# 32x32 turns on VectorE inside the triangular inverses, and a two-pass fp32 output product in the mixer

## Chip, cores and metric
One core of a Trainium2 chip runs one program of 53121 instructions. The time is device microseconds of one execution; lower is better.

## The reference, cut to what matters
Two blocks in sequence on 256 tokens of width 2048, all in float32. The first block's mixer joins an attention half and a state-space half and multiplies them by one output matrix:

```
attn = rms_norm(nsa_attention(...), attn_out_norm)          # 256 x 1024
ssm = mamba2_ssd(...)                                       # 256 x 1024
return jnp.concatenate([attn, ssm], axis=-1) @ w_out        # 2048 x 2048
```

The second block has two recurrent branches (a gated delta rule with 8 heads, and RWKV-7 with 16 heads). The kernel works them in chunks of 128 tokens, and each chunk of each head needs the inverse of a 128x128 lower triangular matrix with a unit diagonal.

## The kernel before, in words
**Products.** Large products keep fp32 accuracy with a faster format: `split` turns a raw 128x1024 weight tile into `whi` (ScalarE, a rounding copy, L280) and `wlo` (VectorE, the remainder, L284), and the activations are kept as a like pair. `mm3` (L291 to L293) adds three products of such halves; `mm2` (L299, L300) does the same with two matmuls where both halves of the activations lie side by side.

**Weights.** `raw` (L261 to L267) loads a tile over SP's queue into four buffers, and while the pool `more` is there, every third tile into two others. `split` has two sets of `whi` and `wlo`, and a third set while the pool `third` is there (it is there in the mixer).

**Order.** The program is written as generators. `fill` takes one step of the product at the head of a queue (load and split one tile, then the matmuls of the tile before it) and, at a set rate, a step of a background generator (`ada_rest`: a 128x1024 tile of the modulation matrix is loaded, VectorE multiplies it in, L355). `weave` mixes such steps into chains of small dependent work. A planner then orders the instructions of each engine; each engine and each DMA queue works in that order.

**Mixer's output product.** `tm` runs over 4 groups of 512 columns. Per group and half it takes 4 weight tiles, each with 2 inner blocks by 2 token halves, so 16 products with 512 columns. The half on the attention's output `aT` runs beside the state-space scan (`ssd`), the half on `mT` after it; `ev_a` and `ev_m` take up the results, `ev_m` also stores them over SP's queue (L684). `chunk_T` turns 128 columns of an activation on TensorE and makes the pair (L444, L445).

**The inverses.** `inverse2` takes two matrices side by side (128x256). It starts from 2x2 squares: mask, turn on TensorE (L1798), subtract from the identity (L1800). Then, for b = 2, 4, 8, 16, 32: two products `lb` by `Y` (L1805), two turns of `Y` on TensorE into the other half of the same bank (L1807), one ScalarE copy of all 512 columns (L1809), a masked block for the next b on GpSimd (L1790), two products of the copies (L1814), and a subtraction into `Y` (L1815). A last step joins the 64x64 halves. It is called 16 times from `rwkv_pair` and 8 times from `gdn_pair`, two calls side by side.

Of the kernel before, what the change touches and what calls it, by code (L numbers as in the profile page):

```python
# [7 lines left out]
F32 = mybir.dt.float32  # L8
F32R = mybir.dt.float32r
I32 = mybir.dt.int32  # L10
U32 = mybir.dt.uint32
AF = mybir.ActivationFunctionType
ALU = mybir.AluOpType
# [5 lines left out]
S = 256  # L19
# [214 lines left out]
class K:  # L234
    def __init__(self, tc, A, at, dbg=None):
        self.tc, self.nc, self.A, self.at, self.dbg_ = tc, tc.nc, A, at, dbg
        self.n = 0
        self.pp, self.queue, self.done, self.bg = [], [], set(), []
        self.bgr, self.bgc = 1.0, 0.0
        self.side, self.later = [], [[] for _ in range(LAG)]  # L240
        self.third, self.ns = None, 0
        self.more, self.nr = None, 0

# [41 lines left out]

    def wt(self, src, n=1024, **kw):
        return self.split(self.raw(src, n), n, **kw)

    def mm3(self, out, shi, slo, mhi, mlo, start, stop):
        mm = self.nc.tensor.matmul  # L290
# [145 lines left out]
    def chunk_T(self, src, dg, hi, lo, scale, half=0):  # L436

        nc = self.nc
        if half == 0:
            self.ctb = self.bank()  # L440
        ps = self.ctb[:, half * S : half * S + S]
        for q in range(2):
            self.turn(ps[:, q * 128 : q * 128 + 128], src[q], dg and dg[q])
        nc.scalar.activation(hi, ps, AF.Copy, scale=scale)  # L444
        nc.vector.scalar_tensor_tensor(lo, ps, scale, hi.bitcast(F32), op0=ALU.mult, op1=ALU.subtract)  # L445

    def chunks_T(self, pool, x, cs, dg, hh, hl, scale, shift):

# [156 lines left out]
    def mixer(self, hp, mx, ax, hT, kvT, qT, xs, ev, scr):  # L605
        nc, tc, A = self.nc, self.tc, self.A
        hh, hl = hT[:2]
# [29 lines left out]
        self.feed(*[self.cm(A["w1cm"], j, hT, lambda j, ps: ev((2 * NP + j + 8) % 12, ps), ("x", j)) for j in range(12 - 2 * NP)])  # L637
        self.feed(*[self.tm(A["w1z"], g, hT, self.gates(xs[2]), ("z", g)) for g in range(2)])
        atp = tc.alloc_tile_pool(name="atp", bufs=1, side="right")
        aT = [self.t(atp, [128, 8, S], F32R) for _ in range(2)]  # L640
        self.until("t320")
        gate = self.t(mx, [128, 2, 48])
        nc.scalar.activation(gate, vtm[:, :, 256:304], AF.Tanh, scale=0.5)
# [13 lines left out]
        nw = self.cp("attn_norm", "cp2")  # L657
        for c in range(8):
            a = [at[:, q, c * 128 : c * 128 + 128] for q in range(2)]
            self.chunk_T(a, None, aT[0][:, c], aT[1][:, c], nw[:, c : c + 1], c % 2)  # L660
        self.dbg("aTd", aT[0].bitcast(F32))
        ax.release()

        xp = tc.alloc_tile_pool(name="x1p", bufs=1)
# [20 lines left out]

        wo = lambda h: [A["wo1"][8 * g + 4 * h + i] for g in range(4) for i in range(4)]
        for g in range(4):
            self.feed(self.tm(wo(0), g, aT, ev_a, nk=8))
        assert not self.side
        self.until(*[("x", j) for j in range(12 - 2 * NP)])  # L690
        self.flush()
        turn, mT = self.ssd(mx, xs, hp)
        self.drain()
        for g in range(4):
            self.feed(self.tm(wo(1), g, mT, ev_m, nk=8))
        self.fill(3)
        for _ in turn:
            pass
        self.dbg("mTd", mT[0].bitcast(F32))
        self.drain()  # L700
        while self.bg:
            self.step_bg()
# [251 lines left out]
    def ssd(self, mx, xs, hp):  # L954

        nc = self.nc
        V, ACT, PL = nc.vector, nc.scalar, nc.gpsimd
        tri = self.cp("tri", "ca")
        xtm, bc, zs = xs
        dt, acs, acsT, ds = self.sd  # L960
        y = zs
        ss = self.t(mx, [128, 4])

        def scan(g, hg, cbT, py):
            h = g * 8 + hg
            pa = self.bank()
            nc.tensor.matmul(pa[:, 0:256], self.ident[:16, h : h + 1].to_broadcast([16, 128]), acsT, start=True, stop=True)
            seg = self.t(mx, [128, 384], tag="seg", bufs=2)
            ACT.activation(seg[:, 0:256], pa[:, 0:256], AF.Relu, scale=-1.0, bias=acs[:, 0, h : h + 1])
            ACT.activation(seg[:, 256:384], pa[:, 128:256], AF.Relu, scale=-1.0, bias=acs[:, 1, h : h + 1])  # L970
            ACT.activation(seg, seg, AF.Exp, scale=-1.0)
            V.scalar_tensor_tensor(seg[:, 0:256], seg[:, 0:256], dt[:, 0, h : h + 1], cbT[:, 0:256], op0=ALU.mult, op1=ALU.mult)
            V.scalar_tensor_tensor(seg[:, 256:384], seg[:, 256:384], dt[:, 1, h : h + 1], cbT[:, 256:384], op0=ALU.mult, op1=ALU.mult)
            yield
            o = slice(hg * 64, hg * 64 + 64)
            xc = slice(h * 64, h * 64 + 64)
            nc.tensor.matmul(py[0][:, o], seg[:, 0:128], xtm[:, 0, xc], start=True, stop=True)
            nc.tensor.matmul(py[1][:, o], seg[:, 128:256], xtm[:, 0, xc], start=True, stop=False)
            nc.tensor.matmul(py[1][:, o], seg[:, 256:384], xtm[:, 1, xc], start=False, stop=True)
            yield  # L980

        def turns(g, mT):
            nw = self.cp("ssm_norm", "cp2")
            for c in range(4 * g, 4 * g + 4):
                a = [y[:, q, c * 128 : c * 128 + 128] for q in range(2)]
                self.chunk_T(a, None, mT[0][:, c], mT[1][:, c], nw[:, c : c + 1], c % 2)
                if c % 2:
                    yield

        for g in range(2):  # L990
            ps = self.bank()
            Bt, Ct = bc[:, g], bc[:, 2 + g]
            nc.tensor.matmul(ps[:, 0:256], Bt[:, 0:128], Ct, start=True, stop=True)
            nc.tensor.matmul(ps[:, 256:384], Bt[:, 128:256], Ct[:, 128:256], start=True, stop=True)
            cbT = self.t(mx, [128, 384], tag="cbT", bufs=2)
            V.tensor_tensor(cbT[:, 0:256], ps[:, 0:256], tri, op=ALU.mult)
            V.tensor_tensor(cbT[:, 256:384], ps[:, 256:384], tri[:, :128], op=ALU.mult)
            py = [self.bank() for _ in range(2)]
            self.fill()
            gens = [scan(g, hg, cbT, py) for hg in range(8)]  # L1000
            if g:
                gens.insert(2, turn)
            self.weave(gens, 1, 0.17)
            self.until(("z", g))
            for q in range(2):
                c = slice(g * 512, g * 512 + 512)
                t1 = self.t(mx, [128, 512], tag="yd", bufs=2)
                PL.tensor_tensor(
                    t1.rearrange("p (h d) -> p h d", h=8), xtm[:, q, c].rearrange("p (h d) -> p h d", h=8),
                    ds[:, g * 8 : g * 8 + 8, None].to_broadcast([128, 8, 64]), op=ALU.mult,  # L1010
                )
                V.tensor_tensor(t1, py[q], t1, op=ALU.add)
                V.tensor_tensor(y[:, q, c], t1, zs[:, q, c], op=ALU.mult)
                ACT.activation(t1, y[:, q, c], AF.Square, accum_out=ss[:, 2 * q + g : 2 * q + g + 1])
            r = self.rstd(mx, ss[:, g::2], 2, 512.0, 4 * EPS)
            y0, y1 = (y[:, q, g * 512 : g * 512 + 512] for q in range(2))
            ACT.activation(y0, y0, AF.Copy, scale=r[:, 0:1])
            V.tensor_scalar(y1, y1, r[:, 1:2], None, op0=ALU.mult)
            if g == 0:
                self.until(("z", 1))  # L1020
                mT = self.pair(hp, 8, "hh")
            turn = turns(g, mT)
        return turn, mT

# [326 lines left out]
    def tm(self, wd, g, hT, evac, key=None, nk=NK):  # L1351

        hh, hl = hT[:2]
        ps = [self.t(self.acc, [128, 512], tag="acc") for _ in range(2)]
        for kp in range(nk // 2):
            hi, lo = self.wt(wd[g * (nk // 2) + kp])
            yield
            for k in range(2):
                kk = 2 * kp + k
                w = slice(k * 512, k * 512 + 512)  # L1360
                for q in range(2):
                    tk = slice(q * 128, q * 128 + 128)
                    self.mm3(ps[q], hh[:, kk, tk], hl[:, kk, tk], hi[:, w], lo[:, w], kk == 0, kk == nk - 1)
        for q in range(2):
            evac(g, q, ps[q])
        self.done.add(key)

    def step_bg(self):
        while self.bg:
# [408 lines left out]
    def inverse2(self, L, res):  # L1778
# [14 lines left out]

        lm, lb = masked(1), masked(2)
        yield
        ps = self.bank()
        for i in range(2):
            nc.tensor.transpose(ps[:, T[i]], lm[:, T[i]], self.ident)  # L1798
        Y = self.r1()
        V.tensor_tensor(v2(Y), id2, v2(ps[:, 0:256]), op=ALU.subtract)  # L1800
        yield
        for b in (2, 4, 8, 16, 32):
            ps = self.bank()
            for i in range(2):
                mm(ps[:, T[i]], lb[:, T[i]], Y[:, T[i]], start=True, stop=True)  # L1805
            for i in range(2):
                nc.tensor.transpose(ps[:, U[i]], Y[:, T[i]], self.ident)  # L1807
            zx = self.r2()
            nc.scalar.activation(zx, ps, AF.Copy)  # L1809
            if b < 32:  # L1810
                lb = masked(2 * b)
            yield
            for i in range(2):
                mm(ps[:, U[i]], zx[:, U[i]], zx[:, T[i]], start=True, stop=True)  # L1814
            V.tensor_tensor(Y, Y, ps[:, 256:512], op=ALU.subtract)  # L1815
            yield
# [496 lines left out]
```

## Time and profile before
| | us |
|---|---|
| median of 3 runs | 3645.67 (3633.72 to 3649.02) |
| the profiled execution | 3638.32, span 3636.3 |
| TensorE busy | 3473.7 |
| VectorE busy | 2570.2 |
| ScalarE busy | 1692.7 |
| GpSimd busy | 397.2 |

Busy times are the union of an engine's instructions. A matmul's own duration holds its way through the array and overlaps with the next one's, so what a matmul costs in a stream is read from the distance between starts. A plain fp32 matmul shows as two matmul records.

### The profile page before, as it was taken

How to read it: one execution, taken by the hardware profiler on the slowest of the kernel's cores; microseconds unless marked ns; L12 is line 12 of the kernel's file. 1: busy time of each engine (PE TensorE's matmuls, PEld its weight loads, DVE VectorE, ACT ScalarE, POOL GpSimd, SP SyncE). 2: the span in 40 equal slices, each digit the busy share in tenths (PEclk: the TensorE clock that was granted, in tenths of full speed). 3: DMA queues.
4: the chain of work that ended last, by engine and by line, in shares of the span. 5: the costliest groups of instructions: out<-in, count | busy, mean ns of one | idle time of the engine just before them, and what ended most of it. 6: DMA issues, size and time to landing. Idle time of an engine off the chain costs nothing. (4 is left out here: it accounts for less than half of the span.)

```text
span 3636.3 us, 53121 instructions
## 1 busy us (share of the span) xinstructions
PE 3473.7 (96%) x19334; PEld 2930.2 (81%) x19334; DVE 2570.2 (71%) x4552; ACT 1692.7 (47%) x2966; POOL 397.2 (11%) x487
## 2 busy tenths in 40 slices
PE   5899988999999999999999998999999999999998
PEld 4888767888998888778887877877888888778887
DVE  7777886798887755565577668989766666665665
ACT  2355544445554444445555554333544445444444
POOL 0000010000000000000000002333223222021310
PEclk7999988999999999999999998999999999999999
DMA  8965776666556865566788755645433433444455
GB/s 334 336 225 194 251 254 209 197 196 202 161 159 207 259 190 188 183 204 206 241 283 285 248 189 202 198 152 188 147 109 112 144 129 106 140 132 151 141 176 189
DMA packets 237298, 710.46 MB, mean 195 GB/s; under 512 B 34091, under 2 KB 61804, under 8 KB 235756
## 3 DMA queue, kind: packets, MB, share of 16 engines
q1 hardware_dynamic: 207564, 672.08, 56.7%
q10 hardware_dynamic: 29472, 34.98, 2.9%
q8 instruction: 152, 2.49, 0.3%
q14 instruction: 110, 0.90, 0.1%
HBM read 673.87 MB, written 32.55 MB: 194 GB/s over the span
## 5 line engine op out<-in xcount | busy, mean ns | idle before, releaser
L284 DVE TENSOR_TENSOR wlo<-raw,whi 128x1024 fp32r<-128x1024 f32 (+1 forms) x973 | 1216.8, 1251 | 595.2 <-ACT whi L280 591.1
L280 ACT ACTIVATE whi<-raw 128x1024 fp32r<-128x1024 f32 (+1 forms) x973 | 1017.7, 1047 | 1252.1 <-PE acc L293 577.2
L299 PE MATMUL acc<-hh,whi 128*128 128x512 f32 x3328 | 1195.2, 400 | 0.7 <-DVE cT L459 0.7
L300 PE MATMUL acc<-hh,wlo 128*128 128x256 f32 x3328 | 939.1, 282 | 7.0 <-DVE wlo L284 7.0
L299 PEld LDWEIGHTS acc<-hh,whi 128*128 128x128 f32 x3328 | 626.2, 188 | 143.3 <-issue 4.5
L300 PEld LDWEIGHTS acc<-hh,wlo 128*128 128x128 f32 x3328 | 629.2, 189 | 13.1 <-DVE wlo L284 11.7
L292 PE MATMUL acc<-wlo,wh 128*128 128x512 f32 x1024 | 402.8, 393 | 6.4 <-DVE wlo L284 5.5
L293 PE MATMUL acc<-whi,wl 128*128 128x512 f32 x1024 | 400.1, 391 | 0.0
L291 PE MATMUL acc<-whi,wh 128*128 128x512 f32 x1024 | 396.9, 391 | 3.3 <-DVE ge L1345 2.8
L291 PE MATMUL acc<-whi,hh 128*128 128x512 f32 (+1 forms) x672 | 273.7, 411 | 3.2 <-DVE r L1345 2.6
L292 PE MATMUL acc<-wlo,hh 128*128 128x512 f32 (+1 forms) x672 | 269.3, 401 | 7.3 <-DVE wlo L284 7.2
L293 PE MATMUL acc<-whi,hh 128*128 128x512 f32 (+1 forms) x672 | 267.0, 398 | 0.0
L292 PEld LDWEIGHTS acc<-wlo,wh 128*128 128x128 f32 x1024 | 192.9, 188 | 56.7 <-DVE wlo L284 16.5
L291 PEld LDWEIGHTS acc<-whi,wh 128*128 128x128 f32 x1024 | 192.7, 188 | 44.9 <-ACT wh L280 3.1
L293 PEld LDWEIGHTS acc<-whi,wl 128*128 128x128 f32 x1024 | 193.1, 189 | 39.5
L293 PE MATMUL acc<-hh,wlo 128*128 128x256 f32 x608 | 181.8, 299 | 13.6 <-DVE wlo L284 13.6
L291 PE MATMUL acc<-hh,whi 128*128 128x256 f32 x608 | 183.4, 302 | 5.2 <-ACT whi L280 3.3
L292 PE MATMUL acc<-hh,whi 128*128 128x256 f32 x608 | 179.0, 295 | 1.0 <-DVE hh L284 1.0
L291 PEld LDWEIGHTS acc<-whi,hh 128*128 128x128 f32 x672 | 129.7, 194 | 41.2 <-issue 11.8
L292 PEld LDWEIGHTS acc<-wlo,hh 128*128 128x128 f32 x672 | 130.8, 195 | 35.4 <-DVE wlo L284 10.9
L293 PEld LDWEIGHTS acc<-whi,hh 128*128 128x128 f32 x672 | 130.0, 194 | 27.4 <-issue 0.3
L1790 POOL TENSOR_TENSOR r<-r,cb 128x256 f32<-128x256 f32 x144 | 133.2, 945 | 162.6 <-DVE r L2123 37.5
(594 smaller groups left out, 5041.9 us busy)
## 6 DMA issues: line engine op xcount, KB each, us to landing
raw<-in_pu_dram SPq DMA_DIRECT2D x256, 512.0 KB, 3.9
raw<-in_pv_dram SPq DMA_DIRECT2D x252, 512.0 KB, 4.3
raw<-in_ada_dram SPq DMA_DIRECT2D x138, 512.0 KB, 5.1
raw<-in_w2gate_dram SPq DMA_DIRECT2D x96, 512.0 KB, 3.6
rawm<-in_ada_dram SPq DMA_DIRECT2D x54, 512.0 KB, 5.3
raw<-in_wo_dram SPq DMA_DIRECT2D x54, 512.0 KB, 4.3
raw<-in_w2br_dram SPq DMA_DIRECT2D x48, 512.0 KB, 3.5
raw<-in_w2g_dram SPq DMA_DIRECT2D x48, 512.0 KB, 3.5
```

What stands on the lines that cost most here:

```text
L280: nc.scalar.activation(hi, src, AF.Copy)
L284: self.lo = e.tensor_sub(lo, src, hi.bitcast(F32)).ins
L291: mm(out, shi, mhi, start=start, stop=False)
L292: mm(out, shi, mlo, start=False, stop=False)
L293: mm(out, slo, mhi, start=False, stop=stop)
L299: mm(out, hi, both, start=start, stop=False)
L300: mm(out[:, S:], lo, both[:, 0], start=False, stop=stop)
L1790: PL.tensor_tensor(v2(lb), v2(L), cb(f"M{b}"), op=ALU.mult)
```

## The change
In `inverse2`, the turns of `lm` and of `Y` go to VectorE's transpose, which turns each 32x32 square in its place; up to b = 32 the matrices that are turned have nothing outside the 32x32 squares on the diagonal. ScalarE copies 256 columns instead of 512. In the mixer's output product, weights and activations stay whole: plain fp32 matmuls on a tile as loaded, with no split, and `chunk_T` makes no remainder. The whole tile is loaded straight into a `whi` or `wlo` buffer (six in turn in the mixer).

```diff
+    def whole(self, src):
+        self.nw = (self.nw + 1) % (6 if self.third else 4)
+        p, n = (self.third, "3") if self.nw > 3 else (self.stg, "")
+        t = self.t(p, [128, 1024], F32R, tag=("whi", "wlo")[self.nw % 2] + n, bufs=1 if n else 2).bitcast(F32)
+        self.nc.sync.dma_start(t, src)
+        return t
...
-        nc.vector.scalar_tensor_tensor(lo, ps, scale, hi.bitcast(F32), op0=ALU.mult, op1=ALU.subtract)
+        if lo is not None:
+            nc.vector.scalar_tensor_tensor(lo, ps, scale, hi.bitcast(F32), op0=ALU.mult, op1=ALU.subtract)
...
-        aT = [self.t(atp, [128, 8, S], F32R) for _ in range(2)]
+        aT = self.t(atp, [128, 8, S])
...
-            self.feed(self.tm(wo(0), g, aT, ev_a, nk=8))
+            self.feed(self.tm_whole(wo(0), g, aT, ev_a, nk=8))
...
-            self.feed(self.tm(wo(1), g, mT, ev_m, nk=8))
+            self.feed(self.tm_whole(wo(1), g, mT, ev_m, nk=8))
...
+    def tm_whole(self, wd, g, hT, evac, nk):
+        ps = [self.t(self.acc, [128, 512], tag="acc") for _ in range(2)]
+        for kp in range(nk // 2):
+            w = self.whole(wd[g * (nk // 2) + kp])
+            yield
+            for k in range(2):
+                kk = 2 * kp + k
+                for q in range(2):
+                    self.nc.tensor.matmul(
+                        ps[q], hT[:, kk, q * 128 : q * 128 + 128], w[:, k * 512 : k * 512 + 512], start=kk == 0, stop=kk == nk - 1
+                    )
+        for q in range(2):
+            evac(g, q, ps[q])
...
-        ps = self.bank()
-        for i in range(2):
-            nc.tensor.transpose(ps[:, T[i]], lm[:, T[i]], self.ident)
+        V.tensor_tensor(v2(lm), id2, v2(lm), op=ALU.subtract)
         Y = self.r1()
-        V.tensor_tensor(v2(Y), id2, v2(ps[:, 0:256]), op=ALU.subtract)
+        V.transpose(Y, lm)
...
-            for i in range(2):
-                nc.tensor.transpose(ps[:, U[i]], Y[:, T[i]], self.ident)
             zx = self.r2()
-            nc.scalar.activation(zx, ps, AF.Copy)
+            nc.scalar.activation(zx[:, 0:256], ps[:, 0:256], AF.Copy)
+            V.transpose(zx[:, 256:512], Y)
```

## Rows read from the trace of the kernel before

**Rows 1.** The page's part 1: busy us, share of the span, instructions.
```profile
PE 3473.7 (96%) x19334; PEld 2930.2 (81%) x19334; DVE 2570.2 (71%) x4552; ACT 1692.7 (47%) x2966; POOL 397.2 (11%) x487
```

**Rows 2.** Windows: length; busy us of PE, PEld, DVE, ACT, POOL; clock; DMA.
```profile
2600.00:2700.00 100.00, 93.50 (x621) 82.05 (x622) 59.06 (x111) 48.23 (x99) 25.69 (x36) 0.98 0.38 117
...
3300.00:3400.00 100.00, 99.59 (x554) 84.22 (x553) 57.45 (x89) 44.92 (x79) 18.64 (x22) 0.98 0.46 153
```

**Rows 3.** Groups by line and form, TensorE: the inverses' products and turns.
```profile
L1805 PE MATMUL sm<-r,r 128*128 128x128 f32 x480 | 75.5, 280 | 1.6 <-DVE r L1800 1.5
...
L1814 PE MATMUL sm<-r 128*128 128x128 f32 x480 | 66.1, 278 | 0.0
...
L1807 PE MATMUL sm<-cs,r 128*128 128x128 f32 x240 | 46.3, 275 | 0.0
...
L1798 PE MATMUL sm<-cs,r 128*128 128x128 f32 x48 | 8.5, 275 | 0.7 <-POOL r L1790 0.5
```

**Rows 4.** Timeline of TensorE near two inverse steps: start us, duration us.
```profile
2605.32 1.05 PE L1814 MATMUL sm<-r 128*128 128x128 f32 x8
2606.13 0.47 PE L299 MATMUL acc<-hh,whi 128*128 128x512 f32 x1
...
2608.98 0.61 PE L1805 MATMUL sm<-r,r 128*128 128x128 f32 x4
...
2610.23 0.47 PE L299 MATMUL acc<-hh,whi 128*128 128x512 f32 x1
```

**Rows 5.** Groups by form: the step's copy and subtraction, a copy half as wide.
```profile
L1809 ACT ACTIVATE r<-sm 128x512 f32<-128x512 f32 x120 | 67.3, 594 | 17.1 <-PE sm L1807 16.4
...
L1815 DVE TENSOR_TENSOR r<-r,sm 128x256 f32<-128x256 f32 x120 | 49.6, 419 | 68.9 <-PE sm L1814 56.8 <-ACT r L2249 3.6 <-ACT r L2054 2.7
...
L1344 ACT ACTIVATE r<-acc 128x256 f32<-128x256 f32 x72 | 26.7, 370 | 1.8 <-PE sm L1805 1.4 <-PE sm L1814 0.4
```

**Rows 6.** Groups by form, VectorE: its only wide transpose before.
```profile
L396 DVE STREAM_TRANSPOSE adr<-adt 128x1024 f32<-128x1024 f32 x2 | 2.5, 1239 | 0.0
```

**Rows 7.** Groups of 420 to 600 us: the output product's split and matmuls.
```profile
L284 DVE TENSOR_TENSOR wlo<-raw,whi 128x1024 fp32r<-128x1024 f32 x26 | 31.6, 1219 | 6.6 <-ACT whi L280 6.6
L292 PE MATMUL acc<-wlo,hh 128*128 128x512 f32 x64 | 29.2, 457 | 6.7 <-DVE wlo L284 6.7
...
L293 PE MATMUL acc<-whi,u 128*128 128x512 f32 x64 | 27.3, 427 | 0.0
```

**Rows 8.** Timeline of TensorE: the output product, from a triple to two later.
```profile
443.71 0.40 PE L291 MATMUL acc<-whi,u 128*128 128x512 f32 x1
...
445.09 0.39 PE L291 MATMUL acc<-whi,u 128*128 128x512 f32 x1
```

**Rows 9.** Timeline of TensorE: plain fp32 matmuls with 512 columns (L745).
```profile
163.64 1.88 PE L745 MATMUL sm<-raw,ca 128*128 128x512 f32 x4
...
165.48 0.28 PE L292 MATMUL acc<-hh,whi 128*128 128x256 f32 x1
165.59 0.28 PE L293 MATMUL acc<-hh,wlo 128*128 128x256 f32 x1
```

**Rows 10.** Timeline of TensorE: long stalls beside the output product, in brackets.
```profile
461.31 0.50 PE L977 MATMUL sm<-u,seg 128*128 128x64 f32 x2 [3.14 <-DVE seg L972]
...
506.81 0.69 PE L432 MATMUL sm<-cs,u 128*128 128x128 f32 x2 [3.53 <-ACT u L1017]
...
557.73 0.80 PE L292 MATMUL acc<-wlo,hh 128*128 128x512 f32 x1 [2.43 <-DVE wlo L284]
```

**Rows 11.** Windows of the output product, columns as in rows 2.
```profile
460.00:470.00 10.00, 8.69 (x37) 7.73 (x37) 9.16 (x13) 4.33 (x8) 2.71 (x2) 0.58 0.45 134
...
550.00:560.00 10.00, 6.95 (x21) 4.29 (x20) 9.56 (x11) 3.71 (x7) 0.00 (x0) 0.86 0.78 271
```

**Rows 12.** Waits of 400 to 640 us: total us, times, longest.
```profile
ACT whi L280 <- DMA raw<-in_wo_dram: 22.7, 9, 5.1
```

**Rows 13.** Waits of VectorE, 2590 to 3490 us, columns as in rows 12.
```profile
DVE wlo L284 <- ACT whi L280: 138.7, 101, 3.8
```

More of the change, by code (lines that the diff above doesn't have):

```diff
@@ L240, in __init__ @@
         self.side, self.later = [], [[] for _ in range(LAG)]
+        self.nw = 0
         self.third, self.ns = None, 0
@@ L659, in mixer @@
             a = [at[:, q, c * 128 : c * 128 + 128] for q in range(2)]
-            self.chunk_T(a, None, aT[0][:, c], aT[1][:, c], nw[:, c : c + 1], c % 2)
-        self.dbg("aTd", aT[0].bitcast(F32))
+            self.chunk_T(a, None, aT[:, c], None, nw[:, c : c + 1], c % 2)
+        self.dbg("aTd", aT)
         ax.release()
@@ L698, in mixer @@
             pass
-        self.dbg("mTd", mT[0].bitcast(F32))
+        self.dbg("mTd", mT)
         self.drain()
@@ L985, in turns @@
                 a = [y[:, q, c * 128 : c * 128 + 128] for q in range(2)]
-                self.chunk_T(a, None, mT[0][:, c], mT[1][:, c], nw[:, c : c + 1], c % 2)
+                self.chunk_T(a, None, mT[:, c], None, nw[:, c : c + 1], c % 2)
                 if c % 2:
@@ L1020, in ssd @@
                 self.until(("z", 1))
-                mT = self.pair(hp, 8, "hh")
+                mT = self.t(hp, [128, 8, S], tag="hh")
             turn = turns(g, mT)
```

## The prediction
> **What bounds the kernel now.** I read the page's totals first: TensorE is busy for 96% of the span, VectorE for 71%, ScalarE for 47% [rows 1]. A busy TensorE can still be waiting inside its pipeline, so I then read windows in the two places that change. Where the inverses run (their first and last matmuls start at about 2600 and 3480 us) TensorE is busy 93.5 us of the first 100 and 99.6 of a later 100, at a granted clock of 0.98, while VectorE has 41 to 43 us free in each [rows 2]. There a microsecond of TensorE work is nearly a microsecond of time. Beside the mixer's output product (420 to 573 us) it is mixed: TensorE is the bound in most of it, but it has long stalls [rows 10], and the clock falls after them: 0.58 in the ten microseconds that hold the first, 0.86 in those that hold the third [rows 11]. The reader should see that a stall there costs twice, once as idle time and once as matmuls at the slower of the two clock levels.
>
> **The inverses: what leaves TensorE.** There are 240 turns in the steps and 48 at the start, 288 in all [rows 3]. Their 275 ns [rows 3] is a latency that overlaps the next matmul; the cost in the stream is the distance between starts. Eight product halves (L1814) push the following L299 from 2605.32 to 2606.13, 0.81 us; eight product halves and four turns push it from 2608.98 to 2610.23, 1.25 us; both times the L299 is the same 0.47 long [rows 4]. So four turns cost 0.44 us, one 0.11, and 288 cost 31.7 us. The Trainium skill, "TensorE: Matmul & The Clock Gate", Part 4: PE-mode transpose, has about 275 ns for a transpose within a kernel; the trace agrees with that as a latency and not as a price in a stream; what it would make of the time stands under the rivals (E).
>
> **What goes to VectorE.** Six transposes of 128x256 per call, 144 in all. The nearest rows bound one: a quarter of the 128x1024 transpose is 0.31 us [rows 6], a two-input operation on 256 columns takes 0.42 [rows 5]. I take the upper, since a narrow operation keeps its fixed part: 144 x 0.42 = 60 us, 7% of the 880 us in which VectorE has some 40% free. The subtraction from the identity stays one operation. It waited for a turn that waited for GpSimd's mask; now it waits for the mask itself, so nothing new is queued behind it. In a step the transpose needs only `Y`, which VectorE has just written, and runs beside TensorE's two products (0.44 us) and ScalarE's copy, which goes from 0.59 us at 512 columns to 0.37 at 256 [rows 5]. It is covered; without that cover it would be 120 x 0.42 = 50 us. The bank of PSUM is used as before. Because TensorE is not busy all of the time, I count 95% of 31.7: **-30 us**, between -25 (stalls take a fifth) and -35 (the shorter chain also takes away stalls).
>
> **The output product: what each product costs.** The groups show 64 products of three matmuls for each half, 128 in all [rows 7]. Two triples take 445.09 - 443.71 = 1.38 us, one 0.69 [rows 8]. A plain fp32 product of the same 512 columns is two matmul records: L745 starts four at 163.64, and the matmul after next starts at 165.48; taking off the 0.11 of the one between, four records take 1.73 us and one product 0.865 [rows 9]. That is 0.175 more than a triple; 128 x 0.175 = **+22.4 us** of TensorE work. The change's second part makes TensorE's work longer, not shorter. The Trainium skill says so too, "FP8 and Floating Point Precision", TensorE Precision Notes: true FP32 is four passes through the array. At the pass length of the triple (0.23 us) four would be 0.92 and the sum +29 us, which would bring the total to 3627; the row has 0.865, so the rule is right in sign and slightly dear.
>
> **What it gives back.** The 32 tiles lose their split: 32 x 1.22 us of VectorE [rows 7] and as many ScalarE copies, and 16 remainders of turned activations. VectorE was not the bound of most of the stage, so this counts only through stalls. TensorE waits 6.7 us for `wlo` in the second half [rows 7]; the splits were late because ScalarE waited 22.7 us for loads of these tiles [rows 12]. The background tiles no longer share their buffers with them, and up to six whole tiles can be loaded ahead, 6 x 4 x 0.865 = 21 us of products. The price of that is that a whole tile's load must wait for the matmuls on the tile that held the buffer before, and behind it in SP's queue stand background tiles and the two stores of each group. I take back 6 of the 6.7. The stalls of 3.14 and 3.53 us are waits for the scan and its normalization [rows 10]; the products queued ahead of them (some seven each by an estimate from the stalls' places) grow by 0.175 each, which covers about 2.5 us. The clock lost 10 x (1 - 0.58) = 4.2 us in the one window and 1.4 in the other [rows 11]; with shorter stalls there is less of this, and I take 5.5 us back over the whole stretch (an estimate from these two windows). The product then costs 22.4 - 6 - 2.5 - 5.5 = **+8.4 us**. Its bounds: +26, if nothing is given back and the first tile's load is exposed once (about 4 us, nearest row the longest wait for a load, 5.1 [rows 12]); and 0, if idle time and cold clock take in all of it.
>
> **Sum.** -30 + 8.4 = -21.6 us. The profiled execution took 3638.3 us and would take 3616.7. It lies 7.4 us under the median of the runs shown; I put the forecast half of that higher, at **3620 us**. A difference under 0.5% (18 us) can hardly be told from none in this kernel, so the forecast stands just outside.
>
> **Rivals.**
> *A, the product pays in full.* The stalls beside it are waits for the scan, for GpSimd and for loads, none of which gets earlier. For it: two of the three long stalls end on something that the change does not touch [rows 10]. Against it: the waits on `wlo` are of the split's making. Sum -30 + 22.4 = -7.6, 3634 us: no measurable change.
> *B, the product is free.* Idle time and the slow clock take in all of the 22.4 us. For it: the idle and cold time around it is about as much, 6.7 + 3.1 + 3.5 us of stalls and the 4.2 and 1.4 us of the two windows [rows 7, 10, 11]. Against it: in the first half TensorE has hardly any stall but the first. Sum -30, 3612 us.
> *C, the other side: the transposes come late on VectorE.* VectorE works in order and stands 138.7 us, 101 times, at a `wlo` that waits for ScalarE [rows 13], 1.4 us each time. A transpose queued behind such a `wlo` delays L1814, where before only TensorE and ScalarE were needed. Against it: the subtraction that makes `Y` is in the same queue just before, so most of such waits are already paid. With 120 steps, the gain is gone when TensorE waits 0.18 us more per step (21.6 / 120), and the kernel is over 0.5% slower from 0.33 us. At 0.35 us: 3620 + 42 = 3662 us.
> *D, the change doesn't take what it says from TensorE,* because the turns filled time in which it would have waited for the chain. Speaking against it is the 99.6% [rows 2]. With half of the 30 us: 3635 us, no measurable change.
> *E, a turn costs TensorE its whole latency* of 275 ns [rows 3]: 288 x 0.275 = 79 us leave, and the sum is 3571 us. Against it stand the distances of rows 4; I give it no chance of note.
>
> **How the numbers follow.** Forecast 0.55 (its own range 3612 to 3630); A 0.18, B 0.16, C 0.05, D 0.06. Faster by over 0.5%: 0.85 of the forecast's cases, since its own range reaches the bound, and B, 0.63. Slower: C beyond its 0.33 us, and something of A and D with a re-planned order, 0.06. The same: the rest, 0.31. The range takes in the bounds: lowest -35 + 0 with the profiled run's own time, 3603; highest -25 + 22 with the median, 3643; outside lie C and the outer ends of the others, 2 in 10.
>
> **What would show each step.** Right: L1798 and L1807 are gone, TensorE's busy time between 2600 us and the end shrinks by 30 us with no new idle time before L1814; 144 transposes of 0.31 to 0.42 us stand on VectorE; the output product shows 256 records of 512 columns, 0.43 us apart; no wait on `wlo` in it, and the stretch from its first to its last matmul grows by about 8 us. Wrong: an L1814 that waits for VectorE (C), a stretch longer by over 20 (A) or by none (B), or stalls on loads of the whole tiles, which would mean that their buffers come free too late.

## The result, and the profile after

The changed kernel took 3599.09 us (median of 5 runs, 3591.01 to 3612.21), the kernel before, run beside it, 3639.79 (median of 5): a ratio of 0.9889, 95% interval 0.9863 to 0.9915, some 41 us. That is faster by over 0.5%, but 4 us under the range that was given, and nearly twice the move of 21.6 us that the sum had. The profiled execution has a span of 3588.9 us.

The page's busy totals of the changed kernel, as in [rows 1]:

```profile
PE 3440.9 (96%) x18918; PEld 2863.4 (80%) x18918; DVE 2580.5 (72%) x4648; ACT 1634.2 (46%) x2934; POOL 394.1 (11%) x487
```

TensorE is busy 33 us less and VectorE 10 us more. Two places give the time back. The inverses' products run from 2581.2 to 3434.1 us, 852.9 us; before, from 2601.0 to 3480.7, 879.7: **-26.8 us**, where -30 was forecast. The output product, from its first matmul (418.94) to the first matmul of the weight product after it (575.19), takes 156.3 us; before it was 419.24 to 592.42, 173.2: **-16.9 us**, where +8.4 was forecast. The forecast's own stretch ends at the last matmul of the output product: it fell from 151.8 us (to 571.08) to 139.0 (to 557.96), so 12.8 of the 16.9 us lie in it and 4.1 behind it. Between the two places and behind the inverses the traces agree within 3 us.

Groups by line and form of the changed kernel, the inverses (answering [rows 3, 5, 6]; L1828 and L1836 are the two products, L1823 and L1831 the new transposes, L1830 the copy, L1837 the subtraction):

```profile
L1836 PE MATMUL sm<-r 128*128 128x128 f32 x480 | 66.9, 278 | 2.0 <-DVE r L1831 1.7 <-ACT whi L281 0.2
L1828 PE MATMUL sm<-r,r 128*128 128x128 f32 x480 | 65.8, 278 | 2.4 <-DVE r L1823 1.4 <-DVE r L1837 1.0
...
L1831 DVE STREAM_TRANSPOSE r<-r 128x256 f32<-128x256 f32 x120 | 51.4, 431 | 0.2
...
L1837 DVE TENSOR_TENSOR r<-r,sm 128x256 f32<-128x256 f32 x120 | 48.7, 414 | 38.8 <-PE sm L1836 33.2 <-ACT r L2271 2.8 <-issue 1.0
...
L1830 ACT ACTIVATE r<-sm 128x256 f32<-128x256 f32 x120 | 41.5, 380 | 21.1 <-PE sm L1828 20.3
...
L1823 DVE STREAM_TRANSPOSE r<-r 128x256 f32<-128x256 f32 x24 | 9.2, 418 | 0.1
```

The turns' groups are gone. The 144 transposes are 60.6 us of VectorE, and TensorE waited for them 1.7 and 1.4 us in all. VectorE's wait for the second product fell from 56.8 us [rows 5] to 33.2.

The output product by windows of 20 us, first the kernel before (columns as in [rows 2]):

```profile
420.00:440.00 20.00, 19.50 (x80) 14.21 (x79) 14.64 (x21) 11.15 (x21) 0.00 (x0) 0.83 0.81 282
440.00:460.00 20.00, 18.17 (x84) 13.21 (x82) 15.66 (x23) 7.91 (x18) 6.38 (x6) 1.00 0.77 252
460.00:480.00 20.00, 18.69 (x78) 15.00 (x79) 15.29 (x23) 9.41 (x18) 2.71 (x2) 0.74 0.63 208
...
500.00:520.00 20.00, 16.07 (x60) 12.05 (x59) 16.81 (x20) 7.87 (x13) 4.36 (x4) 0.83 0.72 244
...
540.00:560.00 20.00, 14.72 (x47) 10.07 (x46) 16.61 (x18) 6.66 (x11) 0.00 (x0) 0.84 0.87 299
560.00:580.00 20.00, 15.02 (x58) 12.32 (x56) 13.70 (x17) 5.46 (x8) 1.51 (x3) 0.76 0.82 297
```

and the changed kernel:

```profile
420.00:440.00 20.00, 20.00 (x74) 10.75 (x73) 13.14 (x20) 6.06 (x15) 0.21 (x1) 1.00 1.03 397
440.00:460.00 20.00, 19.60 (x65) 9.86 (x65) 15.09 (x21) 5.82 (x15) 7.11 (x6) 1.00 0.81 281
460.00:480.00 20.00, 20.00 (x79) 11.07 (x79) 13.47 (x18) 6.80 (x16) 4.57 (x2) 1.00 0.82 288
...
540.00:560.00 20.00, 19.96 (x59) 9.51 (x57) 9.38 (x11) 3.81 (x7) 0.24 (x1) 1.00 0.60 223
560.00:580.00 20.00, 14.68 (x94) 13.27 (x94) 12.86 (x24) 11.65 (x22) 1.05 (x3) 0.91 0.17 60
```

Three things stand in them. TensorE, which before lost 19.8 us of the 160 to idle time, is busy all through to 560 us. Its clock, before at 0.74 to 0.84 in five of these windows, is 1.00 up to 560 us. And the last column: 397 GB/s come in during the first 20 us instead of 282, and the loads are through one window earlier (60 GB/s from 560 us on, where before it is 297).

SP's queue shows what the loads wait for. Its waits from 415 to 580 us (total, times, longest), before:

```profile
SPq L266 <- DVE wlo L284: 58.2, 31, 5.0
SPq L266 <- DVE ada L355: 48.3, 32, 5.1
SPq L684 <- DVE u L682: 16.2, 8, 4.4
```

and after (L295 is the load of a whole tile, L267 that of any other, L694 the stores):

```profile
SPq L295 <- PE acc L1387: 69.5, 21, 5.3
SPq L267 <- DVE wlo L285: 22.4, 2, 17.1
SPq L694 <- DVE u L692: 9.9, 7, 4.8
```

Before, a load went out when VectorE had released a raw buffer, by the remainder of the split or by the background's multiplication. After, the loads of whole tiles wait for TensorE alone, and those of the background hardly at all (the 22.4 us are two loads for later stages).

Before, the loads were late for the split too. ScalarE's wait of [rows 12] is for the tiles in the four buffers; for those in the two others of `raw` it waits as well (415 to 590 us), 32.2 us in all:

```profile
ACT whi L280 <- DMA rawm<-in_wo_dram: 9.5, 3, 5.8
```

The end of the stretch shows the difference. The last load of a background tile for it (SP's queue) and the last work on the tiles, before:

```profile
561.23 0.33 SPq L266 DMA_DIRECT2D raw<-in_ada_dram  x1
...
571.08 0.40 PE L293 MATMUL acc<-whi,hh 128*128 128x512 f32 x1
...
573.32 1.28 DVE L355 SCALAR_TENSOR_TENSOR ada<-raw,u,ada 128x1024 f32<-128x1024 f32 x1
...
574.75 3.54 PE L367 MATMUL sm<-ones,ada 128*128 128x1 f32 x16 [3.27 <-DVE ada L355]
```

and after, with the last load of the output product ahead of it:

```profile
537.68 0.33 SPq L295 DMA_DIRECT2D whi<-in_wo_dram  x1
538.06 0.90 SPq L267 DMA_DIRECT2D raw<-in_ada_dram  x2
...
551.52 3.60 PE L1387 MATMUL acc<-wlo,hh 128*128 128x512 f32 x8
554.96 3.60 PE L1387 MATMUL acc<-whi,hh 128*128 128x512 f32 x8
558.39 1.84 PE L376 MATMUL sm<-ones,ada 128*128 128x1 f32 x16
```

Before, the last background tile is multiplied in only after the last product, and TensorE waits 3.27 us for it. After, the last of these loads go out 23 us earlier, the background is done when the product ends, and TensorE has had work at full clock up to 560 us: there TensorE itself now sets the pace.

### The profile page after: what moved, and what is told of

Its sections match the earlier page's. It is cut to its first block, busy times and chain, and to the rows that moved or that the text cites. A ratio compares the mean times of both kernels' runs of the same rounds, so it can differ in the third digit from the quotient of the medians.

```text
span 3588.9 us, 52403 instructions
## 1 busy us (share of the span) xinstructions
PE 3440.9 (96%) x18918; PEld 2863.4 (80%) x18918; DVE 2580.5 (72%) x4648; ACT 1634.2 (46%) x2934; POOL 394.1 (11%) x487
## 5 line engine op out<-in xcount | busy, mean ns | idle before, releaser
L285 DVE TENSOR_TENSOR wlo<-raw,whi 128x1024 fp32r<-128x1024 f32 (+1 forms) x951 | 1188.0, 1250 | 555.7 <-ACT whi L281 551.3
L281 ACT ACTIVATE whi<-raw 128x1024 fp32r<-128x1024 f32 (+1 forms) x951 | 994.5, 1046 | 1222.4 <-PE acc L302 586.6
L309 PEld LDWEIGHTS acc<-hh,wlo 128*128 128x128 f32 x3328 | 628.2, 189 | 12.1 <-DVE wlo L285 10.7
L300 PE MATMUL acc<-whi,hh 128*128 128x512 f32 (+1 forms) x608 | 247.1, 407 | 4.5 <-DVE r L1355 4.5
L301 PE MATMUL acc<-wlo,hh 128*128 128x512 f32 (+1 forms) x608 | 240.3, 395 | 0.7 <-DVE wlo L285 0.5
L302 PE MATMUL acc<-whi,hh 128*128 128x512 f32 (+1 forms) x608 | 239.6, 394 | 0.0
L364 DVE SCALAR_TENSOR_TENSOR ada<-raw,u,ada 128x1024 f32<-128x1024 f32 x101 | 131.7, 1304 | 21.4 <-DMA raw<-in_ada_dram 20.4
L300 PEld LDWEIGHTS acc<-whi,hh 128*128 128x128 f32 x608 | 116.7, 192 | 36.8 <-issue 14.0
L302 PEld LDWEIGHTS acc<-hh,wlo 128*128 128x128 f32 x608 | 122.9, 202 | 19.6 <-DVE wlo L285 16.5
```

The source lines that it names most:

```text
L281: nc.scalar.activation(hi, src, AF.Copy)
L285: self.lo = e.tensor_sub(lo, src, hi.bitcast(F32)).ins
L300: mm(out, shi, mhi, start=start, stop=False)
L301: mm(out, shi, mlo, start=False, stop=False)
L302: mm(out, slo, mhi, start=False, stop=stop)
L309: mm(out[:, S:], lo, both[:, 0], start=False, stop=stop)
```

## The experiments

In some runs the first output product itself starts later. So each is read by two stretches: the short one used above, and a long one from the last matmul of the attention's heads (400.30 us before, 399.87 after) to the first weight product. The long stretch agrees with the timed runs within some 10 us, and the same old product in "inverses only" is 3.4 us shorter than in "before": a few us in one trace are no sign of anything. "PE busy" is TensorE's busy time in the long one (a slower clock lengthens it too), GB/s the rate of the loads there. Ratios are against the kernel before, run beside each.

| run | ratio (95%) | short, us | long, us | PE busy, us | GB/s |
|---|---|---|---|---|---|
| before | 1 | 173.2 | 192.1 | 169.5 | 256 |
| changed | 0.9889 (0.9863 to 0.9915) | 156.3 | 175.3 | 169.5 | 280 |
| inverses only | 0.992 (0.9902 to 0.9937) | 169.9 | 188.7 | | |
| product only | 0.997 (0.9958 to 0.9982) | 157.4 | 176.4 | 170.6 | 279 |
| first half whole | 0.9979 (0.9966 to 0.9993) | 162.6 | 181.6 | 166.8 | 271 |
| second half whole | 1.0025 (1.0008 to 1.0042) | 178.4 | 197.3 | 176.5 | 250 |
| dead turns | 0.9954 (0.9939 to 0.9968) | 159.5 | 178.5 | | |
| one of three | 1.0009 (0.9993 to 1.0025) | 178.6 | 197.5 | 142.0 | 249 |
| two buffers | 1.0025 (1.0009 to 1.0042) | 179.1 | 202.4 | 184.4 | 243 |
| dead splits | 0.9972 (0.9956 to 0.9988) | 161.8 | 180.8 | 172.5 | 272 |
| triples fed direct | 0.9986 (0.9975 to 0.9998) | 160.0 | 179.1 | 164.6 | 275 |
| four buffers | 0.9961 (0.9947 to 0.9976) | 158.3 | 177.4 | 170.3 | 277 |
| changed again | 0.9886 (0.987 to 0.9902) | 156.5 | 175.5 | | |
| half split | 0.9914 (0.9894 to 0.9934) | 160.9 | 184.9 | 171.2 | 265 |
| split, own buffers | 0.9999 (0.9987 to 1.0012) | 164.8 | 188.6 | 165.6 | 261 |
| whole, shared buffers | 1.0018 (1.0005 to 1.0032) | 175.2 | 194.3 | 178.8 | 253 |
| own buffers and inverses | 0.9928 (0.9909 to 0.9947) | 162.8 | 185.1 | | |

In every row that has them, the long stretch times the rate is 49 MB (192.1 x 256 and 175.3 x 280): the same tiles, the same background. The rate is therefore no second measurement: it does not say whether the loads set the length or follow it.

### The parts alone

The inverses alone, the rest as before (the diff is the part of `inverse2` shown ahead):

> The inverses' part alone; the output product as before. Theory 1 (the two parts add up): between the first and the last product of the inverses the profiles differ by 852.8 - 879.6 = -27 us, so about -27 us, ratio 0.9925, and the stretch of the output product keeps its 173 us from its first matmul to the first matmul of the next projection. Rival (the gain in the mixer came from another order of the planner, whatever the product is): the stretch of the output product gets shorter here too.

Its inverses take 853.0 us, from 2602.6 to 3455.6, and the time falls by 0.8%, 29 us. The short stretch is 169.9 us, 3.3 under that of before with the same product: no more than the spread named above. The product alone:

> The output product alone; the inverses as before. Theory 1: the stretch goes from 173 to 156 us, so about -17 us, ratio 0.995, with the granted clock at 1.00 and hardly a stall in it. Rival (forecast's step: 22 us more work, 14 given back): +8 us, ratio 1.002.

Its inverses take 879.0 us as before, the short stretch 157.4; the time falls by 0.3%, 11 us. 0.992 x 0.997 is 0.989, the whole change: the parts add, and the product gains, where a loss was forecast.

### Half of the product whole

```diff
-            self.feed(self.tm_whole(wo(1), g, mT, ev_m, nk=8))
+            self.feed(self.tm(wo(1), g, mT, ev_m, nk=8))
```

> Whole tiles for the attention half only, the other half split; inverses as before. Theory 1 counts, window by window, what the first half lost before: 3.6 us idle and 8.5 us by the clock, 12 us, against 11.2 us of added work: about -1 us. Rival (plain fp32 matmuls keep the clock up by themselves, so both halves gain alike): about -8 us.

The other way round, `tm` for `wo(0)` and `tm_whole` for `wo(1)`:

> Whole tiles for the state-space half only, the other half split; inverses as before. Theory 1: the second half lost 16 us idle and 11 us by the clock, 27.5 us against 11.2 added: about -16 us. Rival (both halves gain alike): about -8 us.

I had added up idle time and cold clock of each half's windows, and that fails: the first half alone takes 10.5 us off the long stretch, the second alone adds 5.2. In the latter TensorE waits twice for whole tiles, 2.02 us for the first, which is issued only at 507.25 us and needed at 510.9, and 3.12 for one at the end; and the stores stand 45.6 us in SP's queue between 480 and 600 us, ahead of loads. So a half's idle time is not the price of its format. In this run no whole tile was loaded ahead when the second half began. Both halves whole take off 15.7 us, not the 5.3 of the two runs added.

### Turns kept as dead work

```diff
+            for i in range(2):
+                nc.tensor.transpose(ps[:, U[i]], Y[:, T[i]], self.ident)
             zx = self.r2()
             nc.scalar.activation(zx[:, 0:256], ps[:, 0:256], AF.Copy)
```

> The changed kernel with the 240 turns of Y kept on TensorE beside VectorE's transposes; nobody reads their result. Theory (the inverses gained the turns' TensorE work): the stretch from the first to the last product of the inverses goes from 853 back to 875-885 us, 240 x 0.11 = 26 us more, and the time to 3622-3630. Rival (they gained the shorter chain, a copy of 256 columns and one operation less before it): the stretch stays at 853-860 and the time at 3600-3606.

The inverses take 873.4 us (2589.0 to 3462.4), 20.5 more than the changed kernel's 852.9, and the time is 3622.15 us. So 20.5 of the 26.8 us are the work of these 240 turns, 0.085 us each; they stand there as 273 ns apiece:

```profile
L1830 PE MATMUL sm<-cs,r 128*128 128x128 f32 x240 | 45.8, 273 | 0.0
```

The other 6.3 us are left for the 48 turns at the start and the shorter chain, which this run does not take apart. The runs with the old inverses have 875 to 882 us for this stretch, so both figures are good to a few us.

### Two thirds of the matmuls left out

```diff
+                    if one:
+                        self.nc.tensor.matmul(ps[q], hl[:, kk, tk], lo[:, w], start=kk == 0, stop=kk == nk - 1)
```

> The kernel before with two of the three matmuls of each of the output product's 128 products left out (only the remainder times the remainder is computed, so that the split and the wait for wlo stay). 256 matmuls of 0.23 us, 59 us of TensorE work, are gone. If TensorE's work sets the stretch from the first output product to the next weight product (173 us before), it falls to about 114-120 and the time to 3580. Theory (half of what the matmuls do not need is feed and cold clock, and the feed would set the end soon after): the stretch falls by 10 to 30 us only, TensorE waits for wlo more than before, and the clock in it is at or under 0.9.

Neither came: the time did not move (1.0009), and the long stretch grew by 5.4 us with 59 us of matmuls less. Windows of this run:

```profile
460.00:480.00 20.00, 14.90 (x48) 11.12 (x49) 11.30 (x19) 7.91 (x16) 6.36 (x6) 0.50 0.66 201
480.00:500.00 20.00, 17.85 (x51) 12.13 (x49) 17.28 (x22) 10.05 (x19) 3.49 (x2) 0.50 0.69 219
500.00:520.00 20.00, 12.90 (x37) 9.63 (x38) 19.12 (x23) 8.18 (x14) 4.35 (x4) 0.50 0.71 256
...
540.00:560.00 20.00, 12.12 (x24) 6.84 (x24) 16.82 (x17) 5.88 (x9) 0.00 (x0) 0.50 0.90 320
560.00:580.00 20.00, 8.49 (x17) 4.64 (x16) 14.90 (x16) 5.16 (x8) 0.00 (x0) 0.50 0.85 282
```

and TensorE's largest wait in total from 415 to 620 us:

```profile
PE acc L1364 <- DVE wlo L284: 28.8, 17, 3.9
```

TensorE waits for the split instead (28.8 us, before 6.7), and its clock stands at the lower level (0.50). In the old product the matmuls could be two thirds fewer and nothing was gained. Part of that is the clock: what is left of TensorE's work runs at half speed, so this run alone does not say that the loads would have been just as late at full clock. They were as late at the lower one: ScalarE waits 35.9 us for these tiles (28.2 and 7.7), before 32.2.

### Buffers

```diff
-        self.nw = (self.nw + 1) % (6 if self.third else 4)
+        self.nw = (self.nw + 1) % 2
...
+        t = self.t(self.third, [128, 1024], F32R, tag=("whi", "wlo")[self.nw] + "3", bufs=1).bitcast(F32)
```

> The output product whole, the inverses as before, but the whole tiles take turns in two buffers of their own in place of six. Theory (what came back is stall and cold clock, because tiles were ready ahead): TensorE waits for loads again, 5 us or more in total, the clock falls under 0.95 in the stretch, and the stretch goes from 157 us to 165-175, the time from 3626 to 3634-3642. Rival (a stream of plain fp32 matmuls is dense enough by itself, or the freed VectorE is what counts): the stretch stays at 155-160 us and the time at 3622-3630.

With `% 4` and the other four buffers:

> The output product whole, the inverses as before, the whole tiles in four buffers in place of six (two gave 179 us for the stretch, six 157). Theory (it is the tiles that are ready ahead): between the two, 159-168 us, with waits for loads of 1 to 5 us; time 3626-3636. If four are enough: 156-159 us and no wait for loads.

With two buffers the whole gain is gone and more: the short stretch is 179.1 us, beyond the theory's range, the long one is 10 us over that of before, the clock is 0.91 from 420 to 580 us, and TensorE waits for loads:

```profile
PE acc L1387 <- DMA wlo<-in_wo_dram: 9.1, 6, 4.0
...
PE acc L1387 <- DMA whi<-in_wo_dram: 1.9, 4, 0.8
```

With four there is no wait for a load among TensorE's waits of 415 to 620 us, and the stretch is that of six within 1 us. Plain fp32 matmuls are the same in all three. Two buffers are too few and four are enough; the step from four to six is worth nothing here.

### The split kept as dead work

```diff
             w = self.whole(wd[g * (nk // 2) + kp])
+            self.nc.scalar.activation(self.dead[0], w, AF.Copy)
+            self.nc.vector.tensor_sub(self.dead[1], w, self.dead[0].bitcast(F32))
```

> The output product whole, the inverses as before, and the ScalarE copy and the VectorE subtraction of each of the 32 tiles kept as work that nobody reads (1.2 us each on VectorE, 39 us in all). Theory A (the matmuls gained the direct way from the load, without the two engines in between): the stretch stays at 155-162 us, the time at 3622-3631. Theory B (the relief of VectorE counts, because the scan, the background tiles and the normalization are earlier): waits of TensorE for VectorE return, 5 us or more, the clock falls under 0.95 and the stretch goes to 166-176, the time to 3634-3642.

32 copies and 32 subtractions are back (VectorE is busy 133.9 us of 420 to 580, before 130.2), and the time is that of the product alone, 0.9972 against 0.997; the long stretch is 4.4 us longer. So the engine time of the split alone is not what the old product cost; here no matmul waits for it.

### Three matmuls, fed without a split

```diff
+                    self.mm3(ps[q], x, x, self.pairw[0][:, o], self.pairw[1][:, o], kk == 0, kk == nk - 1)
+                    if k + q == 0:
+                        self.nc.tensor.matmul(ps[q][:, 0:8], x.bitcast(F32), w[:, 0:8], start=False, stop=False)
```

> The inverses as before; the output product again in three matmuls per product, but on one pair of weight halves that is made once and is always ready, with the activations in the place of their remainder; each whole tile is still loaded into the six buffers and read by one plain fp32 matmul of 8 columns. The weights' split is left out, and the product is not that of the tiles. If the split's late feed made the old stretch long (theory), the stretch is the 157 us of the plain fp32 product less its dearer matmuls, 157 - 22 = 135 us, 135 to 142 with the small matmuls, with hardly a wait of TensorE, and the time is 3600-3608. Rival (three short matmuls leave TensorE so often waiting for the scan that the clock falls whatever the feed does): the clock stays under 0.95 and the stretch over 150 us.

The theory fails. The short stretch is 160.0 us, not 135 to 142, though the triples are 22 us shorter than the plain fp32 products (the 32 small matmuls take back some 7 of them, which is the expectation's 142). The rival's numbers came, a stretch over 150 us and a clock of 0.93 from 420 to 580 us, but not its reason: TensorE waits for the scan only 1.8 us, and the clock is 0.91 to 1.00 in every window of 20 us up to 560 us. The end of the stretch on TensorE's timeline shows what has taken their place:

```profile
563.86 0.59 PE L1393 MATMUL acc<-wlo,hh 128*128 128x8 f32 x2 [2.95 <-DMA wlo<-in_wo_dram]
...
575.16 3.57 PE L376 MATMUL sm<-ones,ada 128*128 128x1 f32 x16 [6.24 <-DVE ada L364]
```

The last tile of the product is not there yet (2.95 us). The 6.24 us are a wait for VectorE, which after the last product has its results and three background tiles still to do, and which had itself waited 5.55 us for a background load. So late loads reach to the end of the stretch. In SP's queue the stores wait 41.2 us ahead of loads (9.9 in the changed kernel), and the loads are through no sooner than with plain fp32. The work saved was not to be had in this run: against the product alone TensorE's busy time is 6.0 us less and its idle time 8.7 us more in the long stretch (14.5 and 5.8), and part of the work runs at a lower clock (0.58 from 560 to 580 us). The time is 5 us under that of before (0.9986). Whether more could be had with the stores out of the way, no run shows.

### Changed again, and a mixture

> The changed kernel itself, beside the others of this call: 3596-3604 us, ratio 0.987 to 0.991, the sum of the inverses alone (0.992) and the product alone (0.997).

0.9886: the same again. Then every second tile split, in three matmuls:

```diff
+            if kp % 2:
+                hi, lo = self.wt(src)
+            else:
+                w = self.whole(src)
```

> The changed kernel with every second tile of the output product split again and multiplied in three matmuls (64 products at 0.69 in place of 0.865 us, 11 us less of TensorE work); whole tiles take turns in two buffers, split ones in two sets, and the activations keep pairs for the split tiles alone. If a half as frequent split is ready in time: the stretch falls from 156 to 145-150 us and the time to 3588-3594, under the changed kernel. If the waits come back (the clock falls under 0.95, TensorE waits over 5 us for wlo or for loads): 158-170 us, 3600-3612.

By the price of the products 11 us less for TensorE, and 0.9914 where the changed kernel has 0.9886. The waits came back: 4.9 us for the first whole tile, with only two buffers for such tiles, and a clock of 0.91 from 420 to 580 us.

### Split or shared buffers

```diff
+            if own:
+                r = self.t(self.own, [128, 1024], tag="wor", bufs=3)
+                self.nc.sync.dma_start(r, wd[g * (nk // 2) + kp])
+                hi, lo = self.split(r)
```

> The kernel before with the output product split as it was, but its raw tiles loaded into three buffers of their own, so that the background tiles have the six shared ones to themselves. If it was the sharing that held the loads back (SP's queue waits 58 us for the split's remainder and 48 us for the background's VectorE work): the stretch falls from 173 to 155-163 us, SP's waits for the remainder fall under 30 us, and the time is 3620-3630. If the split itself does it (two engines between the load and the matmuls): the stretch stays at 168-176 us and the time at 3633-3641.

And whole tiles, in the raw buffers that the background uses too:

```diff
-            w = self.whole(wd[g * (nk // 2) + kp])
+            w = self.raw(wd[g * (nk // 2) + kp])
```

> The output product whole and plain fp32, the inverses as before, but the whole tiles in the six raw buffers that they share with the background tiles, as before the change; the buffers of the split stand empty. Sharing as the cause: TensorE waits for loads, 5 us or more, and the stretch is 168-178 us, the time 3632-3642. The split as the cause: the stretch is 155-162 us and the time 3622-3630.

Each alone gains nothing in time: 0.9999 and 1.0018. Neither came whole: with the split and own buffers the short stretch, 164.8 us, lies between the two ranges; with whole tiles and shared buffers the stretch is that of sharing as the cause (175.2), but TensorE waits for loads 1.7 us and not 5, and the rest is other waits and the clock. With the split and own buffers SP still waits for the remainders, and ScalarE 31.7 us for the tiles, as before; with whole tiles and shared buffers it waits for TensorE and for the background in one queue. SP's waits from 415 to 590 us, split with own buffers:

```profile
SPq L1358 <- DVE wlo L284: 50.9, 28, 5.0
SPq L266 <- DVE ada L355: 44.2, 26, 5.1
```

and whole with shared buffers:

```profile
SPq L267 <- PE acc L1387: 59.9, 23, 4.8
SPq L267 <- DVE ada L364: 27.6, 20, 3.1
```

In these runs the gain needs both: a buffer that TensorE alone releases, and enough of them that the background does not draw on. A split tile holds its raw buffer until VectorE comes to its remainder. No run gave the split more than three own buffers, so too few buffers and the split itself are not told apart there. Last, that version with the new inverses:

> The run with three own buffers and the split kept, with the inverses of the changed kernel: 27 us less than that run. With sharing as the cause 3593-3603 us, as fast as the changed kernel or a little faster (its matmuls are 22 us shorter); with the split as the cause 3605-3613 us.

0.9928: the inverses' gain (0.992 alone), and nothing more. No version here beats the changed kernel.

## Why the prediction was wrong, point by point

**The inverses: right.** -30 forecast, -26.8 us in the trace and 29 in the timed runs of that part alone. The turn's price was 0.11 us, worked out from distances [rows 4]; kept as dead work 240 turns cost 0.085 us each. So the bounds of -25 and -35 hold, and the larger part of the gain is TensorE's work. At 0.085 us the 288 turns are 24.5 us: that the sum came so near is in part the shorter chain, which it had only in its bound, or the spread between traces.

**VectorE's transposes: right.** 60 us forecast, 60.6 measured, 418 and 431 ns each where 420 was taken. The Trainium skill, "VectorE: DVE Perf Modes", The three transpose paths, has VectorE's transpose in 32x32 blocks at 311 ns for 128x128 in bf16 and a full one on TensorE at 390: VectorE's is the shorter. No run here has bf16. In fp32 a pair takes VectorE 431 ns, and two turns take 0.17 us of TensorE's stream at the price above. Counted so, VectorE's work is the longer, and it pays because it moves the work to an engine with time to spare.

**Rivals C, D, E: refuted.** TensorE waited 3.1 us for the transposes, not 42 (C). The turns did not fill waiting time (D): their dead copies cost 20.5 us. Nor did they cost their 275 ns (E).

**The price of a plain fp32 product: right.** Eight records start 3.44 us before the next eight in the changed kernel (551.52 and 554.96), 0.86 us per product, as [rows 9] had it. The reading that TensorE is the bound in most of the stretch was not right for the old product: with 59 us of matmuls fewer it gained nothing, though at the lower clock. It is right for the new one up to 560 us, where TensorE is busy at full clock. So the 22.4 us are paid, and the miss lies in what comes back for them.

**"What it gives back" is the step that failed.** It took back 14 us, worked out from the longest stalls and two cold windows, and gave 0 as the best bound of the whole product term. That term measured -16.9 us in the trace (-11 in time), so some 39 us came back in the trace. The table's rows "before" and "changed" split them: TensorE's busy time in the long stretch is 169.5 us in both, so the higher clock gave back about what the dearer products took, and idle time fell from 22.6 us to 5.8. Two windows of ten us were a small sample: over the whole of 420 to 580 us the old kernel has 19.8 us of idle and 20 us of cold clock (the sum of 20 x (1 - clock)), which together exceed 22.4 by 17.4. That sum fits here; for the halves it failed.

As far as the runs show, late loads held the old product back: ScalarE waited 32.2 us for tiles of this product, of which the prediction read 22.7 [rows 12] and went on to the waits for `wlo`, where 6.7 us had reached TensorE. The loads were late because SP's queue waited 58.2 us for `wlo` and 48.3 for the background. I had named the cure, six buffers that the background does not share, and priced it as 6 us of waits for `wlo`. Two buffers, shared buffers, and own buffers with the split each lose the gain in time; four or six own ones fed direct have it. These rows point to the place; a price does not follow from them.

**The range** could not hold the result: its lower end took -35 and 0, and left no room for a product that gains. Its upper end took +22 where the product's own bound was +26, which would be 3647.

**Rival B came nearest** (3612 us, the product is free). It named where the time comes from, idle time and the slow clock, at about half of the size: 18.9 us of stalls and cold windows, where the whole stage has 39.8. It did not say what would free them.

**What stays open.** Whether the cold clock of the old product was only a result of the late tiles, or also held it up by itself: no run changed the one without the other. And whether the split with more than three raw buffers of its own would keep pace; no run tried it.

## What to carry to other kernels

Ahead of pricing matmuls in a stage that also streams weights, look at what the DMA queue waits for. If its waits are for buffers, how long a tile holds its buffer may set the stage, and shorter matmuls may then gain nothing (59 us fewer in the old product, some 15 in the new). A format that costs TensorE more but lets one engine release the buffer can then be the faster one, if enough tiles can be ahead (two buffers were too few here, four enough); test it by giving and taking buffers. Sum idle time and the clock's loss over the whole stage and not over its worst windows. Two small reserves that are only worth something together (direct feed, own buffers) look worthless when tried one at a time.

## What was not expected of the hardware

Leaving work out slowed TensorE down: with one matmul of three its granted clock stood at 0.50, the 1.2 GHz level, in five windows of 20 us between 460 and 580 us, with 8.5 to 17.9 us busy in each, and the stretch grew. A VectorE transpose of 128x256 in fp32 takes 431 ns, about as long as a two-input operation of that width (414).
